# Down projection of a hybrid encoder block: activation stationary, weights moving, output position-major

## Chip, cores and metric

The kernel runs on one core of one Trainium2 chip. The metric is the device time of one execution in microseconds (us). The kernel before was timed in three runs: 2042.18 us median, 2039.13 to 2045.5.

## The reference, cut to what matters

One encoder layer over 1024 positions (with 16 meta tokens in front, dropped at the end) and 1024 channels, all in float32:

```python
h = layer_norm(DEEPNORM_ALPHA * h + merged @ w_out[i], ln1_g[i], ln1_b[i])
f = conv_glu_ffn(h, ffn_w_up[i], ffn_conv_w[i], ffn_conv_b[i], ffn_w_down[i])
h = layer_norm(DEEPNORM_ALPHA * h + f, ln2_g[i], ln2_b[i])

def conv_glu_ffn(x, w_up, conv_w, conv_b, w_down):
    a, v = jnp.split(x @ w_up, 2, axis=-1)
    a = causal_dwconv(a, conv_w, conv_b)
    return (jax.nn.silu(a) * v) @ w_down
```

The down projection is the last product: 1024 positions by 2816 hidden rows (22 units of 128) by 1024 channels. What stands ahead of it in the layer (two mixers, the output projection) is not touched by the change.

## The kernel before, in words

**Products.** Every large product is made from three: each operand is split into a high part (a cast to a reduced float type, on ACT, L118) and a low part (the difference, a subtraction on DVE or POOL, L119), and hi*hi, hi*lo and lo*hi are summed in PSUM (L144 to L150). All of them are issued by line 113. Activations are held channel-major: channels on partitions, positions along the row.

**Order.** The program is fully unrolled, and a scheduler places the instructions on each engine's queue by priority, by default in program order; `high_priority(offset=...)` lets a part go that much earlier. Engines work in order. All DMAs are issued by SP, in order; one that has to wait for a buffer holds those behind it.

**Layer norm 1 (L731 to L767) and the up projection (L833 to L942).** The output projection leaves its sums in `acc`, channel-major, in four pieces of positions. For each piece, `out_ln` transposes to position-major (L749), takes statistics, writes the normalised rows `xn` (L753, three buffers of 128 x 1024), transposes back (L760), applies gain and bias per channel into `acc` (L762, L764), and stores the piece to DRAM as `h1_d` (L767; the trace leaves digits out and shows it as h_d<-acc). Then `ops_hi` builds the operands of the up projection, a Strassen scheme of seven products per unit and two halves each, in place in the same tiles of `acc` (L788 to L799), and splits them into `mgh`, `mgl`, `x3h`, `x3l` (eight and four tiles of 8.06 and 12.1 KB per partition). Products one and two read the first four tiles of `mgh` and `mgl`, products four and six the last four. The up projection streams 22 units; each ends with a convolution, a silu and a product, and is stored as `f_d[f]` (L927). Early in it `acc` is loaded again from `h1_d` (L936, L937), as the residual.

**The down projection (L945 to L1051).** The hidden rows go in blocks of 3, 5, 5, 5 and 4 units (`FBLK`). `f_load` (L950) brings a unit back from DRAM and splits it, cast on ACT, subtraction on POOL (on DVE for units 0 to 2). For each output tile `m` of 128 channels the weights `w_down[m, :, f0:f1, :]` are loaded and split (`loadw`, cast on ACT, subtraction on DVE); `down` (L973) makes the weights stationary, moves 512 positions, and adds the sum into `acc` on DVE (L979 for the first block, with the residual's factor; L981 after it). The next block's units are loaded under the current block (L990, L991).

The last block (L993 to L1050) takes the positions in three chunks of 384, 384 and 256 (`CO`, from the back). After a chunk it transposes 128 positions at a time to position-major (L1034; L1020 for the last chunk, part of it early), takes statistics (L177 or L1021, POOL for the power, L184) and applies normalisation, gain and bias in passes of 512 (L1047 to L1049; L1043 and L1044 for the last chunk), then stores.

**Buffers.** `wp` holds two buffers each of raw, high and low weights. The pool `fpe` opens where `mgh` and `mgl` lay, `fp` beyond it; a tile waits for the tiles that it overlaps. PSUM has eight banks, four by `gtile`, four by `stile`.

Of the kernel before, what the change touches and what calls it, by code (L numbers as in the profile page):

```python
# [7 lines left out]
F32 = mybir.dt.float32  # L8
# [6 lines left out]
P = 128  # L15
# [33 lines left out]
FBLK = [(0, 3), (3, 8), (8, 13), (13, 18), (18, 22)]  # L49
FEARLY = {0, 1, 2, 10, 11, 12, 20, 21}  # L50
# [20 lines left out]
def hybrid_block(ctx: ExitStack, tc, x, w_in, w_dt, pool_w, w_ps, w_pp, w_out, w_up, w_down,  # L71
                 pcols, a_log, ln2_g, ln2_b, out):
# [22 lines left out]
    h1_d = dr.tile([KD, P, NT], F32, name="h1_d")  # L95
# [614 lines left out]
    with tc.tile_pool(name="p5", bufs=2, side="right") as p5:  # L710
# [29 lines left out]
        def out_ln(i):  # L740
# [5 lines left out]
            for o in range(0, n, st):  # L746
# [8 lines left out]
                xs.append((xn, o))  # L755
                yield
# [10 lines left out]
            SY.dma_start(h1_d[:, :, a:b].rearrange("k p t -> p k t"), X)  # L767
# [65 lines left out]
    with tc.tile_pool(name="p6", bufs=2, side="right", reuse_waits="tile") as p6:  # L833
# [102 lines left out]
        for m in range(KD):  # L936
            SY.dma_start(acc[:, m, :], h1_d[m])  # L937
# [12 lines left out]
    def f_load(f, fr=None):  # L950
        if fr is None:
            fr = fpe.tile([P, SEQ], F32, tag="fr", name="fr", bufs=2)
        SY.dma_start(fr, f_d[f])
        pl, x, n = (fpe, "e", 3) if f in FEARLY else (fp, "", 7)
        th = pl.tile([P, SEQ], F32R, tag="fh" + x, name="fh", bufs=n)
        tl = pl.tile([P, SEQ], F32R, tag="fl" + x, name="fl", bufs=n)
        split(th, tl, fr, lo_eng=V if f < 3 else None)
        fops[f] = th, tl

    with tc.high_priority(offset=600):  # L960
        for f in range(2):
            f_load(f, pe.tile([P, NT], F32, tag=("fpre", "fv")[f], name="fre", bufs=1)[:, :SEQ])
    wxs.close()
    x3s.close()
    fp = fps.enter_context(tc.tile_pool(name="fp", bufs=1, reuse_waits="tile"))

    with tc.tile_pool(name="p7", bufs=2, reuse_waits="tile") as p6:
        g2 = p6.tile([P, D], F32, name="g2", bufs=1)
        b2 = p6.tile([P, D], F32, name="b2", bufs=1)
        with tc.high_priority(offset=600):  # L970
            f_load(2)

        def down(m, w, K, fs, chunks, first=False):  # L973
            for i, (a, b) in chunks:
                ps = gtile()[:, :b - a]
                mm3(ps, w, 0, K, lambda k, a, b: (fs[k][0][:, a:b], fs[k][1][:, a:b]), a, b)
                o = acc[:, m, a + F0:b + F0]
                if first:
                    V.scalar_tensor_tensor(o, o, ALPHA, ps, ALU.mult, ALU.add)  # L979
                else:  # L980
                    V.tensor_add(o, o, ps)  # L981

        for bi, (f0, f1) in enumerate(FBLK):
            K = f1 - f0
            fs = [fops.pop(f) for f in range(f0, f1)]
            if f1 < NFF:
                n0, n1 = FBLK[bi + 1]
                todo = list(range(n0, n1))
                for m in range(KD):
                    if todo:  # L990
                        f_load(todo.pop(0))  # L991
                    down(m, loadw(w_down[m, :, f0:f1, :], K), K, fs, list(enumerate(CD)), first=bi == 0)
        SY.dma_start(g2, ln2_g.partition_broadcast(P))  # L993
        SY.dma_start(b2, ln2_b.partition_broadcast(P))
        wcs = ExitStack()
        wcp = pool(wcs, "wcp", 1, side="right")
        wc = {m: loadw(w_down[m, :, f0:f1, :], K) for m in range(2)}

        def last_w(m):
            if m not in wc:  # L1000
                wc[m] = (wcp.tile([P, K, P], F32R, name=f"wch{m}"), wcp.tile([P, K, P], F32R, name=f"wcl{m}"))
                raw = wp.tile([P, KD, P], F32, tag="wraw", name="wraw")
# [4 lines left out]
        for i in (2, 1, 0):  # L1007
# [15 lines left out]
            for m in range(KD):  # L1023
                down(m, last_w(m), K, fs, [(i, (a, b))])
                if i == 0 and m == 4:
                    to_tok(range(4))
# [80 lines left out]
```

## Time and profile before

| | |
|---|---|
| median of three runs | 2042.18 us |
| the profiled execution, its own time | 2042.01 us |
| its span (first to last instruction) | 2040.2 us |
| TensorE busy | 1998.2 us, 98% of the span |
| DVE, ACT, POOL busy | 1098.2, 780.3, 641.4 us |
| mean granted TensorE clock | 0.992 of full |
| down projection, from its first matmul to the end | 1773.12 to 2040.2 us |

The span is what the profile shows; the time lies 1.8 us above it. Times in the rows are counted from the span's start. Matmul records overlap: each is longer than the distance to the next one's start. "Idle before" is how long an engine stood before a group or an instruction, and the name behind the arrow is what it stood for. PEclk is the granted TensorE clock, 1.00 being 2.4 GHz.

### The profile page before, as it was taken

To read this page: it belongs to the slowest core of one execution; us is meant where nothing else is said; L and a number is where in the kernel's file an instruction comes from. 1 tells how busy PE (TensorE), PEld (TensorE's weight loads), DVE (VectorE), ACT (ScalarE), POOL (GpSimd) and SP (SyncE) were. 2 spreads that over 40 slices of the span, in tenths; PEclk is the share of its full clock that TensorE was granted. 3 is DMA by queue.
4 is the path that set the end of the run, shared out by engine and by line. 5 is a ranking of instruction groups with operands and counts; after the bars stand their busy time and mean duration, and the time that the engine had idled before them with its cause. 6 is when DMAs were issued, how large, how long until landed. Compare 5 with 4: busy or idle time off the path is not lost.

```text
span 2040.2 us, 33609 instructions
## 1 busy us (share of the span) xinstructions
PE 1998.2 (98%) x13921; PEld 1927.2 (94%) x13921; DVE 1098.2 (54%) x1715; ACT 780.3 (38%) x1150; POOL 641.4 (31%) x421
## 2 busy tenths in 40 slices
PE   7999999999999999999999999989999999999997
PEld 6999999999999999999999999989999999978887
DVE  7746757758646323442233445885645555553337
ACT  4545544544544323323020224664434444422111
POOL 4036657657546511103062320002121111142100
PEclk9999999999999999999999999989999999999999
DMA  6122224224224332225343443552222222443222
GB/s 215 53 79 83 88 63 130 89 81 132 73 78 146 114 120 83 67 67 179 103 147 100 136 137 121 158 178 93 77 80 83 73 88 69 148 156 97 72 55 83
DMA packets 84721, 213.92 MB, mean 105 GB/s; under 512 B 10216, under 2 KB 35656, under 8 KB 84568
## 3 DMA queue, kind: packets, MB, share of 16 engines
q1 hardware_dynamic: 84568, 211.77, 32.5%
q8 instruction: 109, 1.79, 0.4%
q14 instruction: 44, 0.36, 0.1%
HBM read 170.38 MB, written 41.35 MB: 104 GB/s over the span
## 4 chain that ended last, share of the span: by engine, by line
PE 84%; DVE 7%; POOL 3%; ACT 2%; issue 2%; DMA 2%; SPq 0%; DVEq 0%; POOLq 0%; ACTq 0%
PE gps L113 76%; PE sps L113 3%; PE yd L113 1%; POOL acb L425 1%; PE yo L113 1%; DVE wlo L119 1%; PE st L113 1%; DVE Ct L223 1%; ACT whi L118 1%; DVE lnst L177 1%; DMA acb<-ac_d 1%; DVE acb L426 1%; PE xt L433 1%; DVE xy L496 0%; DVE acb L446 0%
## 5 line engine op out<-in xcount | busy, mean ns | idle before, releaser
L113 PE MATMUL gps<-hh,whi 128*128 128x384 f32 (+2 forms) x1536 | 500.1, 326 | 1.1 <-ACT hh L282 1.1
L113 PE MATMUL gps<-hl,whi 128*128 128x384 f32 (+2 forms) x1536 | 495.7, 323 | 4.2 <-POOL hl L285 2.6
L113 PE MATMUL gps<-hh,wlo 128*128 128x384 f32 (+2 forms) x1536 | 492.6, 321 | 0.0
L118 ACT CAST whi<-wraw 128x1024 fp32r<-128x1024 f32 (+3 forms) x246 | 222.3, 905 | 611.7 <-PE gps L113 417.5
L113 PEld LDWEIGHTS gps<-hh,whi 128*128 128x128 f32 x1536 | 290.1, 189 | 8.4 <-issue 4.4
L113 PEld LDWEIGHTS gps<-hl,whi 128*128 128x128 f32 x1536 | 290.9, 189 | 6.9 <-POOL hl L285 4.3
L113 PEld LDWEIGHTS gps<-hh,wlo 128*128 128x128 f32 x1536 | 291.5, 190 | 0.8 <-issue 0.8
L119 DVE TENSOR_TENSOR wlo<-wraw,whi 128x1024 fp32r<-128x1024 f32 (+3 forms) x181 | 210.1, 1163 | 152.3 <-ACT whi L118 151.4
L119 POOL TENSOR_TENSOR wlo<-wraw,whi 128x512 fp32r<-128x512 f32 (+1 forms) x65 | 138.7, 2133 | 436.0 <-ACT whi L118 436.0
L113 PE MATMUL gps<-mgh,wlo 128*128 128x256 f32 (+1 forms) x784 | 222.6, 284 | 4.5 <-DVE wlo L119 2.3
L113 PE MATMUL gps<-mgh,whi 128*128 128x256 f32 (+1 forms) x784 | 223.4, 285 | 1.5 <-ACT whi L118 1.2
L113 PE MATMUL gps<-mgl,whi 128*128 128x256 f32 (+1 forms) x784 | 222.4, 284 | 0.0
L113 PEld LDWEIGHTS gps<-mgh,wlo 128*128 128x128 f32 x784 | 149.2, 190 | 5.2 <-DVE wlo L119 2.5
L113 PEld LDWEIGHTS gps<-mgh,whi 128*128 128x128 f32 x784 | 149.0, 190 | 2.1 <-ACT whi L118 1.6
L113 PE MATMUL gps<-x3h,whi 128*128 128x258 f32 (+1 forms) x528 | 149.1, 282 | 1.3 <-ACT whi L118 0.6
L113 PE MATMUL gps<-x3h,wlo 128*128 128x258 f32 (+1 forms) x528 | 149.1, 282 | 0.7 <-DVE wlo L119 0.7
L113 PEld LDWEIGHTS gps<-mgl,whi 128*128 128x128 f32 x784 | 149.4, 191 | 0.0
L113 PE MATMUL gps<-x3l,whi 128*128 128x258 f32 (+1 forms) x528 | 148.5, 281 | 0.0
L113 PE MATMUL gps<-yh,whi 128*128 128x384 f32 (+3 forms) x448 | 133.7, 298 | 0.0
L113 PE MATMUL gps<-yh,wlo 128*128 128x384 f32 (+3 forms) x448 | 133.5, 298 | 0.0
L113 PE MATMUL gps<-yl,whi 128*128 128x384 f32 (+3 forms) x448 | 133.4, 298 | 0.0
L113 PE MATMUL gps<-fh,wlo 128*128 128x512 f32 (+2 forms) x312 | 121.5, 390 | 0.7 <-DVE wlo L119 0.7
(257 smaller groups left out, 4161.8 us busy)
## 6 DMA issues: line engine op xcount, KB each, us to landing
wraw<-in_w_in SPq DMA_DIRECT2D x64, 512.0 KB, 3.7
wraw<-in_w_up SPq DMA_DIRECT2D x48, 512.0 KB, 3.6
acb<-ac_d SPq DMA_DIRECT2D x32, 512.0 KB, 3.7
wraw<-in_w_out SPq DMA_DIRECT2D x24, 512.0 KB, 3.5
f_d<-sa SPq DMA_DIRECT2D x22, 512.0 KB, 2.6
fr<-f_d SPq DMA_DIRECT2D x20, 512.0 KB, 3.2
y_d<-xy SPq DMA_DIRECT2D x16, 514.0 KB, 5.0
yr<-y_d SPq DMA_DIRECT2D x16, 514.0 KB, 3.5
```

Of the source, the lines that this page charges most:

```text
L113: PE.matmul(ps, lhsT, rhs, start=start, stop=stop, **kw)
L118: (S.copy if hi_eng is None else hi_eng)(hi, src)
L119: (G if lo_eng is None else lo_eng).tensor_sub(lo, src, hi.bitcast(F32))
L177: V.bn_stats(st[:n, i, :], p)
L223: V.scalar_tensor_tensor(dst, pre[:, j:j + T], cw(j), dst, ALU.mult, ALU.add)
L425: G.tensor_tensor(sg, sg, acc_[:L, c, h0:h1, None].to_broadcast([L, HPG, L]), ALU.subtract)
L426: V.tensor_scalar(sg, sg, 0.0, None, ALU.min)
L433: PE.transpose(px[:L, j * P:(j + 1) * P], xy[:, j, a:b], idn)
```

## The change

The down projection is turned round. A unit's activation (128 hidden rows by 1024 positions) is now the stationary operand, 128 positions at a time, and its weights (128 hidden rows by 1024 channels, a new layout made on the host) move, 512 channels at a time. The output is position-major, so the transposes of the last layer norm go. The loop runs over blocks of units, now 3, 5, 3, 3, 3 and 5, over eight blocks of 128 positions, and over two halves of the channels. In the first block all hi*hi come first, then hi*lo, then lo*hi; its sums are copied out of PSUM on ACT, and later ones are added on DVE. `unit_load` loads and splits activation and weights of a unit together, both subtractions on DVE. The residual is no longer loaded into `acc`: layer norm 1 stores its normalised rows before gain and bias (`xn_d`), and in blocks two to four eight blocks of 128 positions are loaded back (`RBLK`), multiplied by gain and factor, and added on DVE. The last block takes statistics from SBUF and normalises in place.

```diff
 WEV = 300
-FBLK = [(0, 3), (3, 8), (8, 13), (13, 18), (18, 22)]
-FEARLY = {0, 1, 2, 10, 11, 12, 20, 21}
+FBLK = [(0, 3), (3, 8), (8, 11), (11, 14), (14, 17), (17, 22)]
+RBLK = {1: {0: 0, 2: 1, 4: 2, 6: 3}, 2: {0: 4, 4: 5}, 3: {0: 6, 4: 7}}
...
     sp_d = dr.tile([KD, P, NT], F32, name="sp_d")
-    h1_d = dr.tile([KD, P, NT], F32, name="h1_d")
+    xn_d = dr.tile([SEQ, D], F32, name="xn_d")
     f_d = [dr.tile([P, SEQ], F32, name=f"f_d{f}") for f in range(NFF)]
...
                 xs.append((xn, o))
+                skip = max(0, F0 - a - o)
+                SY.dma_start(xn_d[a + o + skip - F0:a + o + st - F0, :], xn[skip:st, :])
                 yield
...
                     yield
-            SY.dma_start(h1_d[:, :, a:b].rearrange("k p t -> p k t"), X)
...
             up_act(f, *outs[f])
-        for m in range(KD):
-            SY.dma_start(acc[:, m, :], h1_d[m])
         for f in range(2, NFF):
...
-    def f_load(f, fr=None):
+    def unit_load(u, j, x, n, fr=None):
         if fr is None:
             fr = fpe.tile([P, SEQ], F32, tag="fr", name="fr", bufs=2)
-        SY.dma_start(fr, f_d[f])
-        pl, x, n = (fpe, "e", 3) if f in FEARLY else (fp, "", 7)
-        th = pl.tile([P, SEQ], F32R, tag="fh" + x, name="fh", bufs=n)
-        tl = pl.tile([P, SEQ], F32R, tag="fl" + x, name="fl", bufs=n)
-        split(th, tl, fr, lo_eng=V if f < 3 else None)
-        fops[f] = th, tl
+        SY.dma_start(fr, f_d[u])
+        wr_ = wp.tile([P, D], F32, tag="wraw", name="wraw")
+        SY.dma_start(wr_, w_down[u])
+        pl = fp if n else fpe
+        th = pl.tile([P, SEQ], F32R, tag="fh" + x, name="fh", bufs=n or 3)
+        if x == "e" and j == 0:
+            wh = wp.tile([P, D], F32R, tag="whi", name="dwhi")
+        else:
+            wh = pl.tile([P, D], F32R, tag="wh" + x, name="dwhi", bufs=n or 2)
+        S.copy(th, fr)
+        S.copy(wh, wr_)
+        tl = pl.tile([P, SEQ], F32R, tag="fl" + x, name="fl", bufs=n or 3)
+        if x == "e" and j == 0:
+            wl = wp.tile([P, D], F32R, tag="wlo", name="dwlo")
+        else:
+            wl = pl.tile([P, D], F32R, tag="wl" + x, name="dwlo", bufs=n or 2)
+        V.tensor_sub(tl, fr, th.bitcast(F32))
+        V.tensor_sub(wl, wr_, wh.bitcast(F32))
+        fops[u] = th, tl, wh, wl
...
         for f in range(2):
-            f_load(f, pe.tile([P, NT], F32, tag=("fpre", "fv")[f], name="fre", bufs=1)[:, :SEQ])
+            unit_load(f, f, "e", 0, pe.tile([P, NT], F32, tag=("fpre", "fv")[f], name="fre", bufs=1)[:, :SEQ])
     wxs.close()
...
     fp = fps.enter_context(tc.tile_pool(name="fp", bufs=1, reuse_waits="tile"))
-
-    with tc.tile_pool(name="p7", bufs=2, reuse_waits="tile") as p6:
-        g2 = p6.tile([P, D], F32, name="g2", bufs=1)
-        b2 = p6.tile([P, D], F32, name="b2", bufs=1)
+    act = acc[:, :, :SEQ]
+
+    with tc.tile_pool(name="p7", bufs=2, reuse_waits="tile") as p7:
         with tc.high_priority(offset=600):
-            f_load(2)
-
-        def down(m, w, K, fs, chunks, first=False):
-            for i, (a, b) in chunks:
-                ps = gtile()[:, :b - a]
-                mm3(ps, w, 0, K, lambda k, a, b: (fs[k][0][:, a:b], fs[k][1][:, a:b]), a, b)
-                o = acc[:, m, a + F0:b + F0]
-                if first:
-                    V.scalar_tensor_tensor(o, o, ALPHA, ps, ALU.mult, ALU.add)
-                else:
-                    V.tensor_add(o, o, ps)
-
+            unit_load(2, 2, "e", 0)
+
+        def affine(g, b):
+            gt = p7.tile([P, D], F32, tag="gv", name="gv", bufs=1)
+            bt = p7.tile([P, D], F32, tag="bv", name="bv", bufs=1)
+            SY.dma_start(gt, g.partition_broadcast(P))
+            SY.dma_start(bt, b.partition_broadcast(P))
+            return gt, bt
+
+        g1, b1 = affine(ln1_g, ln1_b)
         for bi, (f0, f1) in enumerate(FBLK):
             K = f1 - f0
-            fs = [fops.pop(f) for f in range(f0, f1)]
-            if f1 < NFF:
-                n0, n1 = FBLK[bi + 1]
-                todo = list(range(n0, n1))
-                for m in range(KD):
-                    if todo:
-                        f_load(todo.pop(0))
-                    down(m, loadw(w_down[m, :, f0:f1, :], K), K, fs, list(enumerate(CD)), first=bi == 0)
-        SY.dma_start(g2, ln2_g.partition_broadcast(P))
-        SY.dma_start(b2, ln2_b.partition_broadcast(P))
-        wcs = ExitStack()
-        wcp = pool(wcs, "wcp", 1, side="right")
-        wc = {m: loadw(w_down[m, :, f0:f1, :], K) for m in range(2)}
-
-        def last_w(m):
-            if m not in wc:
-                wc[m] = (wcp.tile([P, K, P], F32R, name=f"wch{m}"), wcp.tile([P, K, P], F32R, name=f"wcl{m}"))
-                raw = wp.tile([P, KD, P], F32, tag="wraw", name="wraw")
-                SY.dma_start(raw[:, :K, :], w_down[m, :, f0:f1, :])
-                split(*wc[m], raw[:, :K, :], lo_eng=V)
-            return wc[m]
-
-        for i in (2, 1, 0):
-            a, b = CO[i]
-            pas = {}
-
-            def to_tok(ks):
-                for o in range(0, b - a, P):
-                    if o not in pas:
-                        pas[o] = (wcp.tile([P, 2, 6], F32, tag="lnst", name="lnst", bufs=4), [])
-                    st, pa = pas[o]
-                    oo = a + o + F0
-                    q = ks[0] // 4
-                    pt = stile(f"l{q}")
-                    for k in ks:
-                        PE.transpose(pt[:, (k % 4) * P:(k % 4 + 1) * P], acc[:, k, oo:oo + P], idn)
-                    V.bn_stats(st[:, q, :], pt)
-                    pa.append(pt)
-            for m in range(KD):
-                down(m, last_w(m), K, fs, [(i, (a, b))])
-                if i == 0 and m == 4:
-                    to_tok(range(4))
-            if i == 0:
-                to_tok(range(4, 8))
-            for o in range(0, b - a, P):
-                if i:
-                    oo = a + o + F0
-                    pa = [stile("l0"), stile("l1")]
-                    for k in range(KD):
-                        PE.transpose(pa[k // 4][:, (k % 4) * P:(k % 4 + 1) * P], acc[:, k, oo:oo + P], idn)
-                    rr = ln_stats(p6, pa, P)
-                else:
-                    st, pa = pas[o]
-                    rr = ln_stats(p6, [], P, st, raw=True)
-                xn = p6.tile([P, D], F32, tag="sa", name="xn", bufs=2)
-                for q in range(2):
-                    sl = slice(512 * q, 512 * q + 512)
-                    if i == 0:
-                        V.scalar_tensor_tensor(xn[:, sl], pa[q], rr[:, 1:2], g2[:, sl], ALU.subtract, ALU.mult)
-                        V.scalar_tensor_tensor(xn[:, sl], xn[:, sl], rr[:, 0:1], b2[:, sl], ALU.mult, ALU.add)
-                        SY.dma_start(out[a + o:a + o + P, sl], xn[:, sl])
-                        continue
-                    S.activation(xn[:, sl], pa[q], AF.Identity, bias=rr[:, 1:2], scale=rr[:, 0:1])
-                    V.tensor_mul(xn[:, sl], xn[:, sl], g2[:, sl])
-                    V.tensor_add(xn[:, sl], xn[:, sl], b2[:, sl])
-                    SY.dma_start(out[a + o:a + o + P, sl], xn[:, sl])
-        wcs.close()
+            fs = [fops.pop(u) for u in range(f0, f1)]
+            last = f1 == NFF
+            nxt = [] if last else list(range(*FBLK[bi + 1]))
+            if bi == 4:
+                g2, b2 = affine(ln2_g, ln2_b)
+            for pb in range(KD):
+                if nxt:
+                    u = nxt.pop(0)
+                    x, n = (("e", 0), ("n", 5))[(bi + 1) % 2]
+                    unit_load(u, u - FBLK[bi + 1][0], x, n)
+                r = RBLK.get(bi, {}).get(pb)
+                if r is not None:
+                    rs = fp.tile([P, D], F32, tag="rs", name="rs", bufs=2)
+                    SY.dma_start(rs, xn_d[r * P:(r + 1) * P, :])
+                    V.scalar_tensor_tensor(rs, rs, ALPHA, g1, ALU.mult, ALU.mult)
+                    V.scalar_tensor_tensor(rs, b1, ALPHA, rs, ALU.mult, ALU.add)
+                    V.tensor_add(act[:, r, :], act[:, r, :], rs)
+                for h in range(2):
+                    sl = slice(512 * h, 512 * h + 512)
+                    ps = gtile() if h == 0 else stile()
+                    col_ = slice(pb * P, pb * P + P)
+                    seq = [(k, i) for i in range(3) for k in range(K)] if bi == 0 else [(k, i) for k in range(K) for i in range(3)]
+                    for q, (k, i) in enumerate(seq):
+                        th, tl, wh, wl = fs[k]
+                        mm(ps, (th, th, tl)[i][:, col_], (wh, wl, wh)[i][:, sl], q == 0, q == 3 * K - 1)
+                    o = act[:, pb, sl]
+                    if bi == 0:
+                        S.copy(o, ps)
+                    else:
+                        V.tensor_add(o, o, ps)
+                if last:
+                    rr = ln_stats(p7, [act[:, pb, :512], act[:, pb, 512:]], P, raw=True)
+                    for h in range(2):
+                        sl = slice(512 * h, 512 * h + 512)
+                        o = act[:, pb, sl]
+                        V.scalar_tensor_tensor(o, o, rr[:, 1:2], g2[:, sl], ALU.subtract, ALU.mult)
+                        V.scalar_tensor_tensor(o, o, rr[:, 0:1], b2[:, sl], ALU.mult, ALU.add)
+                        SY.dma_start(out[pb * P:(pb + 1) * P, sl], o)
     fps.close()
...
     r["w_up"] = _tiles(np, g["ffn_w_up"][0], KD)
-    r["w_down"] = _tiles(np, g["ffn_w_down"][0], NFF)
+    r["w_down"] = g["ffn_w_down"][0].reshape(NFF, P, D)
     cw = g["ssm_conv_w"][0].reshape(KC, 24, P).transpose(2, 1, 0).reshape(P, 24 * KC)
```

## Rows read from the trace of the kernel before

**Rows 1.** The page, part 1: busy us, share of the span, instructions.

```profile
PE 1998.2 (98%) x13921; PEld 1927.2 (94%) x13921; DVE 1098.2 (54%) x1715; ACT 780.3 (38%) x1150; POOL 641.4 (31%) x421
```

**Rows 2.** Stretches: length, busy PE PEld DVE ACT POOL, PEclk, DMA, GB/s.

```profile
1803.75:1975.07 171.32, 171.32 (x737) 138.81 (x737) 61.59 (x77) 31.75 (x40) 32.35 (x13) 1.00 0.27 86
...
2027.09:2040.20 13.11, 1.49 (x10) 0.75 (x8) 9.53 (x22) 0.00 (x0) 1.06 (x2) 0.66 0.32 120
```

**Rows 3.** PE groups by shape, 1773.12 to 1975.07: count, busy us, mean ns, idle.

```profile
L113 PE MATMUL gps<-fh,whi 128*128 128x512 f32 x288 | 113.4, 395 | 0.0
```

**Rows 4.** Timeline (start us, us, engine, line, operation), PE, up to down.

```profile
1768.83 0.29 PE L113 MATMUL gps<-mgh,whi 128*128 128x256 f32 x1
...
1773.12 0.40 PE L113 MATMUL gps<-fh,whi 128*128 128x512 f32 x1
```

**Rows 5.** Timeline of DVE, POOL and PE, the pause near 1803.

```profile
1790.65 0.55 DVE L119 TENSOR_TENSOR wlo<-wraw,whi 128x384 fp32r<-128x384 f32 x1
...
1800.89 2.39 POOL L119 TENSOR_TENSOR fl<-fr,fh 128x1024 fp32r<-128x1024 f32 x1 [0.34 <-ACT fh L118]
...
1801.25 2.44 DVE L119 TENSOR_TENSOR wlo<-wraw,whi 128x384 fp32r<-128x384 f32 x1 [2.15 <-ACT whi L118]
...
1802.63 0.40 PE L113 MATMUL gps<-fl,whi 128*128 128x512 f32 x1
1803.75 0.50 PE L113 MATMUL gps<-fh,wlo 128*128 128x512 f32 x1 [0.72 <-DVE wlo L119]
```

**Rows 6.** Timeline of PE, transposes after the second position chunk.

```profile
1991.78 2.01 PE L1034 MATMUL l<-idn,acc 128*128 128x128 f32 x16
1993.55 0.42 PE L113 MATMUL gps<-fh,whi 128*128 128x384 f32 x1
```

**Rows 7.** Timeline of PE and DVE, the end of the kernel.

```profile
2026.97 0.28 PE L113 MATMUL gps<-fh,wcl 128*128 128x256 f32 x1
...
2029.98 1.30 DVE L1021 BATCH_NORM_STATS2 lnst<-l 128x6 f32<-128x512 f32 x2 [0.42 <-PE l L1020]
...
2031.68 1.40 DVE L1043 SCALAR_TENSOR_TENSOR xn<-l,lnrr,g 128x512 f32<-128x512 f32 x2
...
2034.32 1.40 DVE L1043 SCALAR_TENSOR_TENSOR xn<-l,lnrr,g 128x512 f32<-128x512 f32 x2
2035.64 1.41 DVE L1044 SCALAR_TENSOR_TENSOR xn<-xn,lnrr,b 128x512 f32<-128x512 f32 x2
```

**Rows 8.** Groups of ACT and DVE, 1773.12 to 1975.07, columns as in rows 3.

```profile
L118 ACT CAST fh<-fr 128x1024 fp32r<-128x1024 f32 x20 | 20.7, 1049 | 34.1 <-DMA fr<-f_d 26.6 <-DMA wraw<-in_w_down 7.5
...
L981 DVE TENSOR_TENSOR acc<-acc,gps 128x512 f32<-128x512 f32 x47 | 32.3, 687 | 104.9 <-PE gps L113 104.9
...
L119 DVE TENSOR_TENSOR fl<-fr,fh 128x1024 fp32r<-128x1024 f32 x1 | 1.2, 1219 | 0.0
```

**Rows 9.** DMA issues: KB each, median us from issue to landing.

```profile
f_d<-sa SPq DMA_DIRECT2D x22, 512.0 KB, 2.6
fr<-f_d SPq DMA_DIRECT2D x20, 512.0 KB, 3.2
```

**Rows 10.** Timeline of ACT and SP, start of the up projection.

```profile
1336.02 0.38 ACT L887 COPY fpre<-gps 128x258 f32<-128x258 f32 x1 [0.36 <-PE lb L760]
...
1341.59 0.33 SPq L839 DMA_DIRECT2D wraw<-in_w_up  x1
```

**Rows 11.** Timeline of SP, DVE and PE, layer norm 1 to up projection.

```profile
1291.30 0.38 SPq L767 DMA_DIRECT2D h_d<-acc  x1
...
1299.24 1.23 DVE L790 TENSOR_TENSOR acc<-acc 128x1032 f32<-128x1032 f32 x1 [2.56 <-DMA h_d<-acc]
...
1306.10 1.22 DVE L119 TENSOR_TENSOR wlo<-wraw,whi 128x1024 fp32r<-128x1024 f32 x1
...
1307.38 0.47 PE L113 MATMUL gps<-mgh,wlo 128*128 128x256 f32 x1 [2.29 <-DVE wlo L119]
```

**Rows 12.** Stretches of 4 us, columns as in rows 2.

```profile
1328.00:1332.00 4.00, 2.74 (x12) 1.95 (x10) 3.11 (x10) 2.62 (x4) 0.92 (x2) 0.50 0.00 0
```

More of the change, by code (lines that the diff above doesn't have):

```diff
@@ L71, in hybrid_block @@
 def hybrid_block(ctx: ExitStack, tc, x, w_in, w_dt, pool_w, w_ps, w_pp, w_out, w_up, w_down,
-                 pcols, a_log, ln2_g, ln2_b, out):
+                 pcols, a_log, ln1_g, ln1_b, ln2_g, ln2_b, out):
     nc = tc.nc
@@ L1087, in prepare @@
         fw, _cols(np, g["ffn_conv_b"][0]), dtb[:, None]], axis=1)
+    r["ln1_g"], r["ln1_b"] = g["ln1_g"][0], g["ln1_b"][0]
     r["a_log"], r["ln2_g"], r["ln2_b"] = g["ssm_a_log"][0], g["ln2_g"][0], g["ln2_b"][0]
```

## The prediction

> **What bounds the kernel now.** I read the page's busy shares first. TensorE is busy for 98% of the span [rows 1], so time can come only from TensorE work that goes away, from pauses of TensorE, and from the stretch after its last matmul.
>
> Next the table of stretches over the down projection [rows 2]. It shows a steady part of 171.3 us in which TensorE never stops and DVE is busy for 61.6 us, and an end of 13.1 us in which TensorE does 1.5 us of work. The reader should see that DVE and ACT have room in the steady part, and that the end belongs to DVE and the output's DMA.
>
> Third, one matmul of 512 columns. Its record is 395 ns long [rows 3], but records overlap; what counts is start to start. From the first down matmul at 1773.12 [rows 4] to the first of the last block at 1975.07 there are 18 x 3 x 8 x 2 = 864 of them in 201.95 us, with one pause of 1803.75 - 1802.63 - 0.23 = 0.89 us [rows 5]: 201.06 / 864 = 0.2327 us each.
>
> **The change, part by part.**
>
> *Matmuls.* Columns streamed stay 22 x 3 x 8 x 1024. Before: 864 matmuls of 512 and 288 of 384 or 256. After: 22 x 3 x 8 x 2 = 1056, all of 512, one weight load each as now. 1056 x 0.2327 = 245.7 us. That the activation now stands and the weights move changes neither shape nor type, so I take the same slot; no row shows this pairing, so a few ns either way per slot stay open (1 ns is 1.1 us).
>
> *Transposes at the end.* 64 transposes of the last layer norm go. Sixteen of them hold TensorE from 1991.78 to 1993.55, 0.11 us each [rows 6]: 64 x 0.11 = 7 us, on the path. They need no term of their own, since I replace the whole stretch from 1773.12 to the end, 267.1 us.
>
> *The end.* Before, 2040.2 - 2026.97 = 13.2 us pass after the start of the last matmul, for two position blocks whose transposes, statistics and four vector passes each come late [rows 7]. After, a block of 128 positions takes 30 matmuls, 7.0 us, and its layer norm runs under the next block's matmuls; only the eighth block's is bare. It costs the rest of the last matmul's record (0.395 - 0.233 = 0.2), one add of 0.69 [rows 8], two statistics passes (1.3), small operations of 0.2 (half of the 0.4 between 2031.28 and 2031.68, which serve two blocks), and four passes of 512 (2034.32 to 2037.05, 2.7) [rows 7]: 5.1 us. From the last pass's end to the span's end 2040.2 - 2037.05 = 3.2 us, the output store, stays. DVE per position block then has 2 x 0.69 + 4.2 = 5.6 us of work in 7.0 us, so it keeps up.
>
> *The start.* The stack of buffers grows: the pool that opens where the up projection's operand tiles lay holds 48 KB per partition instead of 32, four operand tiles of 8.06 KB are freed after the second of seven products, and what lies beyond 33 KB only after the sixth. Laid out in order of first use, the load buffer of unit 2 falls there. The sixth product's first half ends where its second half starts, at 1768.83 [rows 4]; then, at 1769.0, its two loads go out, 0.4 us apart, each landing after 3.2 us [rows 9], about 1772.6; two casts of 1.05 [rows 8] end at 1774.7. TensorE wants them at 1773.12 + 2 x 0.23 = 1773.6, so it waits 1.1 us, and three matmuls later about 0.6 us more for the weight's low part on DVE (1.22). I take 1.7 us. Lower end 0, as now; upper end 5.5, when the buffer comes free only with the last up matmul (3.2 + 1.05 + 1.22). I take the middle because the buffer sizes give it.
>
> *Unit loads.* Every unit of 128 hidden rows now brings 1 MB: activation and weight rows, two casts on ACT (2.1 us), two subtractions on DVE (2.4 us) [rows 8]. One unit from issue to ready is 3.6 + 2.1 + 1.2 = 6.9 us and two are in flight. A block of three units lasts 3 x 3 x 8 x 2 x 0.2327 = 33.5 us, five units 55.8. Five units are loaded under a block of three twice, for the second and for the sixth block, placed at the heads of the first five position blocks: the fifth's work stands behind the fourth's sums, 4 x 4.2 = 16.8 us in, and ends at 24. Cost 0, hidden by 33.5 us. In the first block ACT also takes over 16 copies out of PSUM; 258 columns cost 0.38 [rows 10], so 512 about 0.6: 9.6 + 10.5 = 20 of 33.5 us. If the cover goes, the next block's start is late; that is a rival below.
>
> *Residual.* Eight rows-blocks of stored layer norm come back with three DVE passes of 1.22 each, 29 us in all. In the busiest block with them, the third, DVE has 16 x 0.69 + 3 x 2.44 + 2 x 3.66 = 25.6 of 33.5 us. Cost 0. They queue ahead of sums out of PSUM, which TensorE misses only after eight half-blocks, 17 us.
>
> *GpSimd leaves.* 19 subtractions on GpSimd go to DVE. Row: the DVE subtraction of 384 columns at 1801.25 took 2.44 us beside a GpSimd one of 2.39 us from 1800.89, against 0.55 us at 1790.65, and TensorE's one pause of 0.89 us ended on it [rows 5]. So the pause goes with GpSimd's work, and DVE's subtractions cost their undisturbed price; that is already in the 0.2327. The Trainium skill, "SBUF — State Buffer", section "SBUF: two separate sides", says DVE instructions with two SBUF inputs and GpSimd share a port pair that one holds for a whole instruction. By that rule the trace agrees, 2.44 against 0.55 us. If the pause had another cause, the sum would be 0.9 us higher.
>
> *Layer norm 1.* Its output was stored from the very tiles (1 MB, issued at 1291.30) that the operand building then overwrites; DVE stood 2.56 us until 1299.24 for that read, and is packed from there, so that a weight's low part at 1306.10 came late and TensorE idled 2.29 us until 1307.38 [rows 11]. The change stores the tile before gain and bias instead, ten stores on the same SP queue, so this wait goes. TensorE's 2.3 us are on the path: gain 2.3. Bounds: 0 if another wait takes the place, and about 6 if the low clock that follows goes too. The eight reloads of that output (4 MB) leave the SP queue early in the up projection; eight loads of the same 4 MB come later, plus 1 MB of broadcast gain and bias. Neither has anything on the path.
>
> **The sum.** Down to the end: 1.7 + 245.7 + 5.1 + 3.2 = 255.7 against 267.1, gain 11.4. With 2.3 of layer norm 1: 13.7. Span 2040.2 - 13.7 = 2026.5; the profiled execution is 2042.01, 1.8 over its span and 0.2 under the median of 2042.18, so 2028.3 us.
>
> **Rivals.**
>
> *A, more comes back at layer norm 1.* The granted clock stood at half, 1.2 GHz, from 1328 to 1332 and beyond, after TensorE had stopped and started there, with 2.7 us busy in 4 [rows 12]. If the earlier DVE keeps it at 2.4 GHz, some 4 us more, and with a bare start of 0 another 1.7: 2022. Against: that stretch waits on ACT and DVE, not on matmuls. 0.12.
>
> *B, loads one after another.* If the two in flight don't overlap, a unit costs 3.6 + 2.1 + 2.4 = 8.1 us, five 40.5 against 33.5 + 2.8 (the fifth is wanted 12 matmuls into its block): 4.2 late, twice: 2036.7. For it: casts on ACT wait in order, ahead of the copies that free PSUM. 0.10.
>
> *C, slower.* Same place, worse price: each unit is also held by the queue order (SP's loads behind a wait, ACT's casts behind TensorE's sums). It decides at a unit time u from 2 x (5u - 36.3) = 20, u = 9.3 us, where the run is over 0.3% slower; at 10 us it gives 2028 + 27 = 2056. Against: in the trace loads land in 3.2 us [rows 9] with the SP queue free. 0.09.
>
> *W, a new wait at layer norm 1.* The tiles that held the normalised rows are reused by the up projection's outputs; ACT's first such copy waited for the last transposes until 1336.02, and now waits for a store of 2.6 us [rows 9] as well. In queue order that is about even; if the store stands behind the weight load issued at 1341.59 [rows 10], ACT is held 1341.6 + 2.6 - 1336.0 = 8.2 us, and with the 2.3 not gained: 2039. 0.07.
>
> **How the numbers follow.** The forecast, 2028.3, has the remaining 0.62, its own range 2025 to 2032 by the start's bounds. A measurement of this kernel tells about 0.3%, 6 us, from no change. Faster by more (under 2036): forecast and A, 0.74, and a part of B and W, 0.07: 0.81. Within: the rest of B and W, 0.10. Slower: C, 0.09. The range takes in A and reaches to the near side of B and W: 2021.5 to 2037.5.
>
> **What would show it.** Right: matmul starts 0.233 us apart in the whole down projection; no pause at the five block starts; a pause of 1 to 3 us at its first matmuls; about 8 us from the last matmul to the end; no GpSimd work there but the powers; no DVE wait on a store near 1297, and TensorE's pause near 1305 gone. Wrong: waits on unit loads at the second or the last block (B, C); the copy into the first up output waiting for a store (W); slots longer than 0.246 us, which alone would eat the gain.

## The result and the profile after

The changed kernel takes 2051.57 us (median of 4 runs, 2049.01 to 2052.34) against 2041.13 us before (median of 4): ratio 1.0052, 95% interval 1.0039 to 1.0064. It is slower by half a per cent, where 2028.3 and faster had been forecast. The profiled execution took 2052.06 us, its span 2050.0.

Part 1 of the page of the changed kernel answers to [rows 1]:

```profile
PE 1990.4 (97%) x13761; PEld 1915.3 (93%) x13761; DVE 1135.7 (55%) x1732; ACT 776.1 (38%) x1136; POOL 596.7 (29%) x402
```

TensorE's share has fallen by a point, so time was lost in pauses more than in matmuls. **Where** is read from one start time. The first down matmul stood at 1773.12 before [rows 4]. Here is TensorE's timeline of the changed kernel from it on (`dwhi` and `dwlo` are the high and low part of the down weights, `fh` and `fl` those of the activation, `gps` and `sps` PSUM tiles):

```profile
1800.45 0.62 PE L113 MATMUL gps<-dwhi,fh 128*128 128x512 f32 x2
...
1800.91 0.62 PE L113 MATMUL sps<-dwhi,fh 128*128 128x512 f32 x2
```

So 1800.45 - 1773.12 = 27.3 us were lost ahead of the down projection; from there to the span's end it is 2050.0 - 1800.45 = 249.6 us, against 267.1 before: 17.5 gained. The two make the 9.8 us between the spans (2050.0 against 2040.2).

**The down projection** did better than the prediction said. The chain of waits of the changed kernel shows its blocks of five units and of three:

```profile
1885.14 3.40 PE sps L113 x15
...
1898.94 2.08 PE sps L113 x9
...
1923.86 2.04 PE sps L113 x9
```

Fifteen matmuls in 3.40 us are 0.2267 us each, nine in 2.08 are 0.231; over the whole stage (2041.75 - 1800.45) / 1055 = 0.2287, against 0.2327 before. The table of stretches over a steady part and the end answers to [rows 2] (columns: stretch, its length, busy time of each engine with instructions, granted clock, DMA share, GB/s):

```profile
1814.00:1980.00 166.00, 166.00 (x727) 136.03 (x726) 109.94 (x122) 41.90 (x48) 0.00 (x0) 1.00 0.40 135
2042.00:2050.00 8.00, 0.14 (x1) 0.00 (x0) 4.57 (x9) 0.00 (x0) 0.55 (x1) 0.83 0.17 66
```

TensorE never stops, DVE is busy for 66% instead of 36% and has room, GpSimd does nothing. The end, [rows 7] before, in the timeline of the changed kernel:

```profile
2041.75 0.39 PE L113 MATMUL sps<-dwhi,fl 128*128 128x512 f32 x1
2042.18 0.69 DVE L1023 TENSOR_TENSOR acc<-acc,sps 128x512 f32<-128x512 f32 x1 [0.79 <-PE sps L113]
2042.90 0.69 DVE L177 BATCH_NORM_STATS2 lnst<-acc 128x6 f32<-128x512 f32 x1
2043.63 0.21 DVE L179 BATCH_NORM_AGGREGATE lnmv<-lnst 128x2 f32<-128x12 f32 x1
...
2044.12 1.44 DVE L1029 SCALAR_TENSOR_TENSOR acc<-acc,lnrr,gv 128x512 f32<-128x512 f32 x2
...
2045.48 1.40 DVE L1030 SCALAR_TENSOR_TENSOR acc<-acc,lnrr,bv 128x512 f32<-128x512 f32 x2
```

One position block is left, and 2050.0 - 2041.75 = 8.3 us pass, as summed (5.1 + 3.2).

**Layer norm 1** is where the 27 us went. TensorE's timeline of the changed kernel there (in brackets the idle time before and what ended it):

```profile
1290.36 1.94 PE L749 MATMUL l<-idn,acc 128*86 128x128 f32 x8 [15.02 <-ACT xn L753]
...
1312.31 0.90 PE L749 MATMUL l<-idn,acc 128*128 128x128 f32 x6 [3.37 <-ACT acc L766]
...
1328.30 0.55 PE L113 MATMUL gps<-mgh,whi 128*128 128x256 f32 x1 [3.93 <-DVE acc L737]
```

ACT's timeline in the first of these pauses:

```profile
1283.86 1.04 ACT L118 CAST whi<-wraw 128x1024 fp32r<-128x1024 f32 x1 [15.33 <-DMA wraw<-in_w_out]
```

The chain of waits of the changed kernel, its two longest pieces there:

```profile
1263.32 20.52 DMA wraw<-in_w_out
...
1299.31 11.34 DMA wraw<-in_w_out
```

TensorE stands for 15 us; ACT, which is to write the next rows, has a weight cast (line 118) in front of them in its order, and that waits for a load of 512 KB which takes 20.5 us. The median load of that weight takes 3.6 on the page. The order of issue in SP's queue shows what is in front of it:

```profile
1258.81 0.33 SPq L720 DMA_DIRECT2D wraw<-in_w_out  x1
1259.23 3.99 SPq L757 DMA_DIRECT2D xn_d<-xn  x3
1263.32 25.93 SPq L720 DMA_DIRECT2D wraw<-in_w_out  x4
1290.99 0.26 SPq L757 DMA_DIRECT2D xn_d<-xn  x1
```

Three of the new stores. What they do is seen in the table of stretches, first of the kernel before, then of the changed one: around the issue of the third store, in the 3 us after it, and in a part of the pause:

```profile
1276.00:1283.00 7.00, 6.91 (x59) 6.70 (x59) 5.29 (x15) 5.34 (x7) 1.64 (x3) 1.00 0.60 154
...
1262.00:1264.00 2.00, 2.00 (x23) 2.00 (x22) 1.07 (x2) 1.99 (x4) 0.00 (x0) 1.00 0.13 53
1264.00:1267.00 3.00, 3.00 (x30) 3.00 (x29) 1.76 (x3) 2.46 (x5) 0.00 (x0) 1.00 0.64 205
...
1276.00:1283.00 7.00, 0.00 (x0) 0.00 (x0) 0.00 (x0) 0.00 (x0) 0.00 (x0) 0.73 0.13 53
```

In the pause no engine works, and the DMA engines' mean busy share is 0.13, which is 2 of 16, at 53 GB/s. It is the same from 1262 to 1264, with TensorE at work. The load goes out at 1263.32, and from 1264 to 1267 all transfers move 205 x 3 = 615 thousand bytes, of which 53 x 3 = 159 thousand are what two engines move. The other 456 thousand are about 14 sixteenths of the load (524 thousand): they have moved by 1267, and what the load still waits for is on the two engines that the stores hold. The page's part on DMA issues lists the ten stores by size: four of 512 KB (128 partitions), landing after 2.6 us, five of 344 KB (86) and one of 328 KB (82), since a piece of 258 positions is normalised in three chunks of 86, the first without its four leading rows. The first three hold 328 + 344 + 344 = 1016 KB, or 1.04 MB: at 53 GB/s that is 19.6 us, about the time the load took.

**The theory (T1)**: a store of 86 or 82 partitions is carried by two DMA engines only; three in a row occupy those two for 20 us, and the load behind them, which has a share on all 16, is not complete before. The Trainium skill, "DMA: Bandwidth & Descriptors", section "Why a DMA increments its semaphore by 16 and not by 1", says that the number of engines is the largest up to 16 that divides the slowest dimension of both sides, and that these are the lowest-numbered ones: 2 for 86 and 82, 16 for 128 or 80. By that rule the trace agrees, 0.13 busy; which two engines they are, no run here shows. Rivals: **T2**, SP's queue order holds the loads behind stores that wait for their rows; **T3**, the writes as such.

Not all of the 27.3 us are pauses. TensorE stands for 32.5 us between 1240 and 1400, against 10.5 before; that is 22. The other 5 go with a lower granted clock behind the pauses: from 1290 to 1300, where TensorE is busy for 9.6 us, it is 0.68 on average, and was 1.00 before.

### The profile page after: what moved, and what is told of

It is laid out like the page before. It is cut to its first block, busy times and chain, and to the rows that moved or that the text cites. A ratio compares the mean times of both kernels' runs of the same rounds, so it can differ in the third digit from the quotient of the medians.

```text
span 2050.0 us, 33186 instructions
## 1 busy us (share of the span) xinstructions
PE 1990.4 (97%) x13761; PEld 1915.3 (93%) x13761; DVE 1135.7 (55%) x1732; ACT 776.1 (38%) x1136; POOL 596.7 (29%) x402
## 4 chain that ended last, share of the span: by engine, by line
PE 85%; DVE 6%; DMA 3%; POOL 3%; issue 2%; ACT 1%; SPq 0%; DVEq 0%; POOLq 0%; ACTq 0%
PE gps L113 71%; PE sps L113 9%; DMA wraw<-in_w_out 2%; PE yd L113 1%; POOL acb L425 1%; DVE Ct L223 1%; PE yo L113 1%; PE st L113 1%; DVE acb L426 1%; DVE wlo L119 1%; DVE xy L496 1%; PE xt L433 1%; DVE acb L446 1%; ACT whi L118 0%; DMA xin<-in_x 0%
## 5 line engine op out<-in xcount | busy, mean ns | idle before, releaser
L118 ACT CAST whi<-wraw 128x1024 fp32r<-128x1024 f32 x212 | 199.0, 942 | 517.7 <-PE gps L113 298.2
L119 DVE TENSOR_TENSOR wlo<-wraw,whi 128x1024 fp32r<-128x1024 f32 (+1 forms) x147 | 171.1, 1167 | 168.6 <-ACT whi L118 167.8
L184 POOL TENSOR_TENSOR lnrr<-lnmv,mhalf 128x1 f32<-128x1 f32 (+2 forms) x27 | 19.2, 712 | 404.2 <-DVE lnrr L183 250.7
```

Of the source, the lines that this page charges most:

```text
L118: (S.copy if hi_eng is None else hi_eng)(hi, src)
L119: (G if lo_eng is None else lo_eng).tensor_sub(lo, src, hi.bitcast(F32))
L184: G.tensor_tensor(rr[:n, 0:1], mv[:n, 1:2], mhalf[:n, 0:1], ALU.pow)
```

## The experiments

Any edit at layer norm 1 makes the program's order of instructions be planned anew around it; I take differences of a few us there as open for that reason. Groups of these runs were taken on different chips, each with its own runs of the kernel before; so times of different groups are best compared by their ratios to it, which follow the medians.

**E1. Each 86- or 82-row store cut into 80 rows and the rest**, at the same place of the queue.

```
-  SY.dma_start(xn_d[a + o + skip - F0:a + o + st - F0, :], xn[skip:st, :])
+  for r0, r1 in ((skip, st),) if st == P else ((skip, skip + 80), (skip + 80, st)):
+      SY.dma_start(xn_d[a + o + r0 - F0:a + o + r1 - F0, :], xn[r0:r1, :])
```

> Six of the ten stores of layer norm 1 hold 86 or 82 partitions; here each of them goes out as two, 80 partitions and the rest, at the same place of the same queue. Theory T1: a store of 86 or 82 partitions keeps only two of the 16 DMA engines busy (0.13 of them at 51 to 55 GB/s in 1268 to 1283), three in a row hold those two for 20 us, and the weight load behind them, which needs all 16, lands 20.5 us late. Then the load behind the stores lands in under 6 us, TensorE's 15 us pause goes, the first down matmul starts at about 1773 instead of 1800.45, and the time falls by 26 to 29 us to 2023 to 2026. Rival T2: the place of the stores in SP's queue holds the load (a store that waits for its rows lets nothing past it); then the cut changes nothing, 2050 to 2053. Rival T3: ten writes of the rows to DRAM cost this much however they are cut: also 2050 to 2053.

Measured: 2026.3 us, ratio to before 0.9933 (0.9919 to 0.9946). 25 us come back through the cut of six stores; T2 and T3 fall, since number, bytes and place are what they were or more. The load behind the first three stores lands after 4.8 us instead of 20.5, and the first down matmul stands at 1773.91. The stretch that was empty, in this kernel:

```profile
1276.00:1283.00 7.00, 6.70 (x60) 6.50 (x58) 4.34 (x9) 3.80 (x6) 0.55 (x1) 1.00 0.69 214
```

**E2. The same stores cut into halves of 43 (41)**: as E1, with `(skip + st) // 2` for `skip + 80`.

> The same six stores, each cut into two halves of 43 or 41 partitions. T1: neither 43 nor 41 has a divisor up to 16 but 1, so that one engine carries it all; the mean DMA share of the stretch falls from 0.13 to about 0.07 and three stores take about 40 us instead of 20; the load behind them lands some 20 us later still, and the time grows by 15 to 35 us over the changed kernel's, to 2067 to 2087. T2 and T3: the cut changes nothing, 2050 to 2053. If it were only the size of a store that counts, smaller ones would be faster.

Measured: 2083.5 us, 1.0208 (1.0192 to 1.0224). The table of stretches of this kernel, while the six half stores run:

```profile
1270.00:1283.00 13.00, 7.16 (x59) 6.43 (x57) 4.35 (x12) 2.06 (x3) 1.09 (x2) 0.85 0.06 26
```

Half the share and half the rate: one engine. Smaller stores are slower, and how many engines carry them goes by the count of partitions, as the rule has it. Something else grows here, which the expectation had not: SP itself stands at the issues, the six half stores take it 22.7 us (4.0 for the three whole ones), and the load behind them goes out only at 1282.57. So the price of this cut is not the engines' alone; why SP stands was not tried.

**E3. The whole stores issued from ACT** (`S.dma_start` for `SY.dma_start`).

> The ten stores whole, 86 partitions as in the changed kernel, but issued from ACT, so that no load stands behind them in SP's queue. T2: the loads go out at once and the 27 us come back, 2023 to 2027, with each load landing in under 6 us. T1 with engines that serve one queue to its end: still 2047 to 2053. T1 with engines that share themselves between two queues: the two engines still carry three stores for 20 us, the load gets half of each beside them and lands in some 6 to 10 us instead of 20, and 15 to 25 us come back, 2027 to 2037; the stretch then still shows a DMA share near 0.13 between loads.

Measured: 2039.3 us, 0.9985 (0.9975 to 0.9994). 12 of 27 us come back, 2 us outside the range that T1 gave with engines shared between queues. The rest of that expectation came: the loads of the output projection's weights beside the stores land after 6.4 us (median of the ten from 1259 to 1305), and between them the share is 0.13 again:

```profile
1267.00:1270.00 3.00, 3.00 (x30) 3.00 (x30) 1.61 (x3) 1.97 (x3) 0.00 (x0) 1.00 0.13 52
```

E6 divides what is missing: the cut stores from ACT take 2033.0, so by the medians 2039.3 - 2033.0 = 6.3 us go with the two engines even with a queue of their own, and 6.7 with issuing from ACT (2033.0 - 2026.3). By the ratios it is 4.9 and 5.7, and each of the three programs has its own order of instructions.

**E4. The down projection alone changed**: the old store kept, no rows stored.

```
-  SY.dma_start(xn_d[a + o + skip - F0:a + o + st - F0, :], xn[skip:st, :])
...
+  SY.dma_start(h1_d[:, :, a:b].rearrange("k p t -> p k t"), X)
...
-  SY.dma_start(rs, xn_d[r * P:(r + 1) * P, :])
+  SY.dma_start(rs, x_in[r * P:(r + 1) * P, :])
```

> Layer norm 1 stores its output as the kernel before does (1 MB after the gain and bias) and no normalised rows; the down projection is the changed one and reads rows of the input where the residual's rows would be (that part of the result is left out). So the down projection alone is changed. From the trace of the changed kernel, its down projection takes 249.6 us against 267.1, so 2041.1 - 17.5 = 2023.6: I expect 2022 to 2026, with TensorE's pause of 2.3 us near 1305 there as before. If the stores of the rows have nothing to do with the loss: about 2050. Against the first run of this call it shows whether the store that the change removed cost 2.3 us: then the first run is 2 to 3 us faster than this one.

Measured: 2023.63 us, 0.9911 (0.9898 to 0.9925): 18.7 us under the kernel before of the same group (2042.31). In its trace the first down matmul stands at 1772.75 and 249.6 us follow, as in the changed kernel, so the 17.5 us of the down projection are there; that the median hits 2023.6 is luck of the medians. The pause is there too, 2.06 us before 1308.04. One expectation missed: E1 was to be 2 to 3 us faster than this run, and by the medians it is 2.7 slower.

**E5. Neither store** (E4 without its added store at layer norm 1).

> Neither store of layer norm 1, the old one nor the new one; the residual's rows are read from the input again, and that part of the result is left out. It measures what the old store itself cost. If TensorE's pause of 2.3 us near 1305 is due to the old store alone, as the prediction had it, this is 2 to 4 us faster than the run with the old store (2023.63): 2019.5 to 2021.5, and DVE's wait of 2.56 us on that store is gone. If another wait stands behind it (a weight's cast, the packed DVE), 2022.5 to 2024.5.

Measured: 2023.7 us, 0.9917 (0.9901 to 0.9932): no gain over E4. DVE's wait on the store is gone, but TensorE's timeline of this kernel has two other pauses in place of the one [rows 11]:

```profile
1308.33 0.36 PE L113 MATMUL gps<-mgh,whi 128*128 128x256 f32 x1 [1.94 <-DVE lnmv L181]
...
1315.89 0.58 PE L113 MATMUL gps<-mgh,whi 128*128 128x258 f32 x1 [2.73 <-DVE lnmv L181]
```

They end on DVE's statistics, so the store was not the only thing that DVE was late for. The matmuls, too, stand in another order in this program than in E4's, so the run doesn't price the wait by itself.

**E6. The cut stores from ACT** (E1 with `S.dma_start`).

> The cut stores (80 partitions and the rest) issued from ACT, right behind the two passes that write the rows, so that no load stands behind them on SP and SP waits for no rows. If what the cut version still loses against the run with the old store (2026.3 to 2023.63) is the loads standing behind stores that wait on SP: 2022 to 2024. If ACT pays for the issues (16 of some 0.3 us, on an engine that the normalisation waits for): 2026 to 2031.

Measured: 2033.0 us, 0.9961 (0.9946 to 0.9976), 6.7 slower than E1 by the medians and beyond both expectations. The sixteen issues make 16 x 0.34 = 5.5 us of ACT's queue; what the rest is, and whether the new order of instructions has a part in it, stays open.

**E7. The cut stores late**, all of a piece behind its last transposes, where the old store was issued.

```
+  if k == KD - 1:
+      for xn, o in xs:
+          skip = max(0, F0 - a - o)
+          for r0, r1 in ((skip, st),) if st == P else ((skip, skip + 80), (skip + 80, st)):
+              SY.dma_start(xn_d[a + o + r0 - F0:a + o + r1 - F0, :], xn[r0:r1, :])
```

> The cut stores, all of a piece together behind its last transposes, where the kernel before issued its own store. The loads then stand in front, as before; but the buffers of the normalised rows come free later for the next piece. If the stores' place among the loads is what is left: 2022 to 2024.5. If the next piece's rows wait for the buffers (some 3 to 8 us of stores): 2027 to 2032.

Measured: 2020.38 us, 0.9904 (0.9883 to 0.9925): the lowest median of all, 31 us under the changed kernel and below both expectations. From E4 and E5 it can't be told by the intervals, and E1's (0.9919 to 0.9946) just meets its own. The first down matmul stands at 1769.21, 3.9 us earlier than before. TensorE's pauses from 1240 to 1400 add up to 9.0 us against 10.5 before, and the granted clock is higher in two stretches. First the kernel before, then this one:

```profile
1300.00:1320.00 20.00, 16.94 (x125) 16.23 (x124) 18.51 (x31) 12.38 (x18) 1.12 (x2) 0.91 0.26 80
1328.00:1340.00 12.00, 10.10 (x53) 9.11 (x52) 8.88 (x17) 9.37 (x16) 0.92 (x2) 0.57 0.30 105
...
1300.00:1320.00 20.00, 18.17 (x143) 16.82 (x142) 17.95 (x33) 12.97 (x21) 2.23 (x2) 1.00 0.41 133
1328.00:1340.00 12.00, 10.75 (x73) 9.55 (x73) 10.99 (x16) 11.02 (x18) 0.00 (x0) 0.86 0.43 139
```

**E11. Late, but whole** (E7 without the cut).

> The rows' stores late, behind the last transposes of their piece as in the fastest version so far (2020.4), but whole, with 86 and 82 partitions. Theory T1 (two engines carry such a store): three of them together hold two engines for 20 us from there, and the next weight load behind them lands late: 2035 to 2055. Theory P (the place was the loss, not the number of engines): 2019 to 2023.

Measured: 2045.5 us, 1.0009 (1.0000 to 1.0018), 25 us over E7 by the medians (the first down matmul stands 24.8 us later), and 6 under the changed kernel. Theory P falls: at the later place the loss is there all the same. TensorE's timeline has the pauses again, 10.69 us before 1281.31 and 7.31 us before 1313.24.

**E12. The kernel before with the ten stores added**, which nothing reads.

```
+  skip = max(0, F0 - a - o)
+  SY.dma_start(xn_d[a + o + skip - F0:a + o + st - F0, :], xn[skip:st, :])
```

> The kernel before, which keeps its own store and its own down projection, with the ten stores of normalised rows added that nothing reads. T1: the loss belongs to these stores alone, not to what the change did elsewhere: the same 15 us pause of TensorE near 1275 and 24 to 30 us more than before, 2065 to 2072. If the loss needed the missing store or the changed down projection: within 5 us of 2041.

Measured: 2070.9 us against 2043.2, 1.0127 (1.011 to 1.0145): 27.7 us more, the loss of the changed kernel with nothing else changed, and its pause in TensorE's timeline:

```profile
1295.72 0.65 PE L750 MATMUL l<-idn,acc 128*86 128x128 f32 x2 [15.73 <-ACT xn L754]
```

**E8. GpSimd back in the down projection**, in E1's kernel: `(V if u < 3 else G).tensor_sub(tl, ...)`.

> The cut version with the activation's low parts of units 3 to 21 subtracted on GpSimd again, as in the kernel before, beside all else of the changed down projection. Theory G (GpSimd slows DVE): DVE's subtractions of 1024 columns beside it go from 1.2 to some 2.4 us or more, but TensorE does not miss them (DVE has room), so within 1 us of 2026.3. Theory G2: GpSimd was also behind the longer spacing of the matmuls before (0.2327 us against 0.2267 in the changed kernel's blocks of five): the spacing there goes back to 0.23 or more and the time to 2029 to 2032.

Measured: 2029.8 us, 0.9944 (0.9927 to 0.9961), 3.5 us over E1 by the medians, not to be told from E1's 0.9933 by the intervals. The time lies where G2 had it, but the spacing stays (15 matmuls in 3.40 us), so G2 falls. The lines of the down projection, first of this kernel:

```profile
L113 PE MATMUL gps<-dwlo,fh 128*128 128x512 f32 x156 | 58.5, 392 | 1.1 <-DVE dwlo L970 1.1
...
L969 POOL TENSOR_TENSOR fl<-fr,fh 128x1024 fp32r<-128x1024 f32 x19 | 52.4, 2770 | 124.3 <-ACT fh L962 99.3 <-PE sps L113 24.8
...
L970 DVE TENSOR_TENSOR dwlo<-wraw,dwhi 128x1024 fp32r<-128x1024 f32 x21 | 40.3, 1928 | 15.3 <-ACT dwhi L963 15.3
```

and of E1's:

```profile
L970 DVE TENSOR_TENSOR dwlo<-wraw,dwhi 128x1024 fp32r<-128x1024 f32 x21 | 25.5, 1219 | 2.3 <-ACT dwhi L963 2.2
```

The mean DVE subtraction goes from 1.22 to 1.93 us, and TensorE waits 1.1 us for one of them, which G had not expected.

**E10. GpSimd out of the kernel before's down projection**: `split(th, tl, fr, lo_eng=V)` for all units, nothing else.

> The kernel before with the activation's low parts subtracted on DVE for all units, so that GpSimd leaves its down projection, and nothing else. The prediction's step: its pause of 0.89 us near 1803 ended on a DVE subtraction slowed by GpSimd to 2.44 us; without GpSimd that subtraction takes 0.55 us and the pause is gone, and the spacing of 0.2327 us stays: 2040 to 2041. If GpSimd was also behind the spacing (0.2327 against 0.2267 to 0.231 in the changed kernel): 2034 to 2038. If the pause has another cause: unchanged, 2041 to 2042.

Measured: 2040.1 us, 0.9990 (0.9980 to 1.0000). TensorE has no pause left from 1770 to 1990, the weight's subtractions on DVE take 0.75 us in the mean instead of 1.12, and matmuls still start 0.232 us apart: the prediction's step holds. The subtraction on which the pause had ended, in DVE's timeline of this kernel:

```profile
1800.56 0.55 DVE L119 TENSOR_TENSOR wlo<-wraw,whi 128x384 fp32r<-128x384 f32 x1
```

**E9. Low tiles without loads**, in E1's kernel.

```
-  fs = [fops.pop(u) for u in range(f0, f1)]
+  fs = [fops[u] for u in (14, 15, 16, 14, 15)] if bi == 5 else [fops[u] for u in range(f0, f1)]
...
-  nxt = [] if last else list(range(*FBLK[bi + 1]))
+  nxt = [] if last or bi == 4 else list(range(*FBLK[bi + 1]))
```

> In the changed down projection matmuls start 0.2267 us apart in some blocks and 0.231 us in others; the slower ones are the blocks whose operand tiles lie in the lower part of the buffer memory (every second block), where the loads' buffers lie too. Here the last five units are not loaded, and the last block uses the three units of the block before it again (the sums of five units are left out and of five taken twice), so two blocks run on the low tiles with no unit load beside them. If the address of the operands sets the spacing: 0.231 us in both blocks (18 matmuls in 4.16 us or 15 in 3.47). If it is the loads, casts and subtractions beside them: 0.2267 (15 in 3.40). The time itself says nothing else here; about 2020 to 2027.

Measured: 2027.9 us in one run. The chain of waits of this kernel, a block on high tiles, then the two on low ones:

```profile
1923.29 2.04 PE sps L113 x9
...
1931.49 2.08 PE sps L113 x9
...
1980.05 3.47 PE sps L113 x15
```

3.47 / 15 = 0.2313 us, with no unit loads beside it: the spacing goes with where the operand tiles lie, not with the unit loads. The place of the activation's tile alone doesn't set it: in the kernel before, units 0 to 2 lie on low tiles and units 3 to 7 on high ones, their weights always in `wp`, and matmuls start 0.232 us apart in both blocks. Why the place matters was not tried.

## Why the prediction was wrong

**The step that failed** is layer norm 1: "The change stores the tile before gain and bias instead, ten stores on the same SP queue, so this wait goes." The ten stores got no term in the sum, and so a price of nothing, without a reason. Where a store had a price, in rival W, it was the landing of 512 KB from 128 partitions, 2.6 us [rows 9]. Six of the ten have 86 or 82 partitions, take 6.6 us each at the rate of two engines (344 KB at 53 GB/s), and stand in front of weight loads on the path. Where the sum had a gain of 2.3 us stood a loss of 27.3. E1, E2, E11 and E12 show the cause from four sides: the cut mends it, a worse cut more than doubles it, the place alone doesn't mend it, and the stores bring it to the kernel before.

**The rivals** missed it too. W had a store of 2.6 us in a queue that holds up reused tiles; the queue was right, the store's price and the one who waits were not. B and C put the loss at the unit loads, and TensorE has no pause between its first and last down matmul. A was the nearest to what the change can do, 2022 against 2020.4 in E7: there the bare start is 0 and a part of the clock that it named is back (0.86 against 0.57 from 1328 to 1340). That the numbers lie so close is partly luck, since E7 also has the shorter spacing of the matmuls, 4.2 us, which A had not.

**The gain of 2.3 us** is not shown as such. DVE waits for no store in E1, and the pause that had cost 2.29 us is 0.80 there (before 1306.82); but all pauses from 1240 to 1400 add up to 13.2 us, against 10.5 before. Without any store (E5) other pauses took the place of that one, the lower bound of 0 that I had named. E7 gains 3.9 us ahead of the down projection, but with an order of its own.

**The terms of the down projection:** 249.6 us against 255.7 summed. *Matmuls*: 1056 x 0.2287 = 241.5, not 245.7; the spacing of the kernel before, 0.2327, was carried over, with a few ns open either way, and the blocks of 13 of the 22 units run on tiles with a shorter one (E9). *Start*: 0, not 1.7. The third unit was about as late as I had it: the cast of its activation ends 1801.89 - 1800.45 = 1.4 us behind the first down matmul, 1.6 in the sum. In ACT's timeline of the changed kernel:

```profile
1800.84 1.05 ACT L961 CAST fh<-fr 128x1024 fp32r<-128x1024 f32 x1 [1.83 <-DMA fr<-f_d]
```

But TensorE took the products of other position blocks with the first two units meanwhile, each into a PSUM tile of its own, as the pairs in its timeline near 1800 show. *End*: 8.3, as summed. *Loads, residual*: hidden, as said, though a unit's two loads land after 4.4 and 4.6 us on the page instead of the 3.2 that I took. *GpSimd*: the pause of 0.89 us goes with it (E10).

With the stores cut (E1) the forecast would have been 2 us off by the median and 3.3 by the profiled execution's span (2023.2 against 2026.5). That closeness is luck, since two misses of opposite sign make it: the span's end comes 6.4 us earlier after the first down matmul than summed (2023.2 - 1773.91 = 249.3 against 255.7), and that matmul itself stands 0.8 us later than before instead of 2.3 earlier.

## What to carry to other kernels

Look at the partition count of every new DMA before its bytes: in these runs 86 or 82 partitions were carried at 53 GB/s, 43 at 26, and cut to 80 and a rest they were out of the way. The slow stores cost time here through what stood behind them in the queue and shared their engines. Cutting them gave 25 us back (E1); a place behind the loads is worth some 6 by the medians, with the cut (E7 against E1) and without it (E11 against the changed kernel), which is little more than the open few us of a new order. A busy share that is a small multiple of one sixteenth, with all engines idle, is a sign to look for.

## What was not expected of the hardware

- The load of 16 engines behind three stores of two engines took 20.5 us instead of 3.6, though 14 engines had nothing to do for the last of them (share 0.13 from 1276 to 1283).
- Matmuls of one shape start 0.2267 or 0.231 us apart, about 2%, according to the block of operand tiles that they read (E9); the cause is open.
- From a queue of their own (E3) the two-engine stores still cost some 5 or 6 us over cut ones (E6), and a load beside them lands after 6.4 us instead of 3.6.
